# Small results of the sample's attention move to the three PSUM banks of the prompt's row maxima, and their own bank becomes a third bank of the prompt's scores

## The chip, the cores and the metric

The kernel runs on one core of a Trainium2 chip. The metric is the device time of one execution in microseconds (us), and of several runs the median. The core has TensorE (PE in the profile; its weight loads are a row of their own, PEld), VectorE (DVE), ScalarE (ACT), GpSimd (POOL) and SyncE (SP), whose queue issues nearly all transfers. Each engine works through its instructions in the order in which the program has them. A matrix product is written to PSUM, which has eight banks of 128 partitions by 512 fp32 numbers, and VectorE or ScalarE reads it from there.

## What is computed

One inference step of a small hybrid decoder, for a prompt of 2048 new tokens and for a sample batch of 8 sequences with 8 new tokens each and 4096 cached positions: a recurrent layer (RG-LRU), a shared key, value and forget stream, and one attention layer with 16 heads of 64. The change lies in the attention, whose core is

```
def fox_block(q, k, v, cq, ck, q_pos, k_pos):
    s = jnp.einsum('bqhd,bkhd->bhqk', q, k).astype(jnp.float32) * (HEAD_DIM ** -0.5)
    s = s + jnp.swapaxes(cq, 1, 2)[:, :, :, None] - jnp.swapaxes(ck, 1, 2)[:, :, None, :]
    mask = k_pos[None, :] <= q_pos[:, None]
    s = jnp.where(mask[None, None], s, -jnp.inf)
    p = jax.nn.softmax(s, axis=-1)
    return jnp.einsum('bhqk,bkhd->bqhd', p.astype(v.dtype), v)
```

For the prompt, k and v are its own 2048 rows. For the sample they are the cached pages (each of 128 rows, found through a page table) and the 8 new rows.

## The kernel before

**Stages.** The recurrent layer, the projections to q, k, v and the gate, and, from about 1708 us of the profiled execution on, the prompt's attention (the generator `attention`). It ends at about 2890 us, and the output projection (`project`) follows. The sample's attention (`decode`) runs beside the projections and beside the prompt's attention, up to about 2725 us: a `Side` object advances its generator by a share of the cost that the main generator reports, so the two are traced alternately. The framework's scheduler then makes each engine's order out of the traced order and its own model of when operands and buffers come free. That order is fixed in the program.

**The prompt's attention.** A unit is a head and a block of 512 queries, 64 units in all; even heads take their blocks in the order 0 to 3, odd heads in the order 3 to 0, so that a head has 4, 8, 12 and 16 key tiles, or the reverse: 640 key tiles in all. Four kinds of work make up a unit:

- *Maxima* (`top`, L1415 to L1419). For 128 queries and up to 512 keys a rough product goes to a bank `sx` (L1415). VectorE reduces it to a row maximum, with L1417, or with L1419 on the diagonal, which also adds the mask. A block's maxima are turned by a transpose (`mps`, L1432), and ScalarE writes them, negated, into rows 96 to 99 of the query tile `qbt` (L1434). Maxima are traced up to 18 key tiles (`LEAD`) ahead of the scores.
- *Scores* (`st`). Per key tile, two products into one bank: L1552 (`ka`, `qa`) and L1553 (`kbt`, `qbt`), which brings in the maxima and so needs the ScalarE rows. On the diagonal a third (L1555) adds the mask. ScalarE takes the exponential (L1561), into a tile `p`, or, for the first key tile of a unit, into a tile `acc`.
- *Products* (`ops`, L1572) of `p` and the values, after each four key tiles; GpSimd adds the `p` tiles up into `acc` (L106, the line of a helper).
- *Totals* (`tot`, L1465). After each four units, the four `acc` tiles are summed over partitions, which ends their use. There are 5 `acc` tiles. A total, a head's end (`rp`, L1489) and `mps` use banks of the tag `sx` too.

**The sample's attention.** A turn is one sequence and 8 heads, 16 turns in all, of which some ten lie beside the prompt's attention. Per turn, key pages arrive in `raw`, VectorE transposes them to `ktr` (L1168), and TensorE makes four sets of scores `dS` of 32 products each (L1136) and a small one for the new rows (L1151). VectorE subtracts the forget sums (`sc`, L106) and takes the maximum `gmx` (L1142). One bank `dm` then goes through a transpose (L1188), two VectorE steps (L1190, L1191), a product (L1192) and a VectorE copy (L1194). `dsum` (L1214) holds the softmax sums and `dres` (L1274) the turned result. The products with the value pages accumulate in a bank of their own, `dO` (L1246).

**Banks beside the prompt's attention.** Tag `st`: two. Tag `sx`: three. `ops`: one. Tag `d`: one, used in turn by `dS`, `dm`, `dsum` and `dres` through `bank`. Tag `o`: one, for `dO`. When `decode` has ended (`dec_done`), scores take the banks `d` and `o` as well, in the function `scores_bank`. A tag's tiles are given out in the traced order, each when the tile that had the bank is read out.

Of the kernel before, what the change touches and what calls it, by code (L numbers as in the profile page):

```python
# [11 lines left out]
F32 = mybir.dt.float32  # L12
# [8 lines left out]
P = 128  # L21
# [64 lines left out]
def tile_hawk_fox(  # L86
# [135 lines left out]
    psum = {}  # L222
# [810 lines left out]
    def decode(es, turns, nraw, nktr, ahead):  # L1033
# [26 lines left out]
        last, qbs = [], {}  # L1060

        def bank(name, tag="d"):
            return psum["dec"].tile([P, 512], F32, name=name, tag=tag, bufs=1)

        def spare():
# [52 lines left out]
        def keys(t, xs):  # L1118
# [11 lines left out]
            def scores(g, pp, kt):  # L1130

                sp = bank("dS", "d" if ahead or pp == 0 else "o")

                def score(h, x, a):
                    blk = (h * 2 + x) * 32
                    return T.matmul(sp[a * 32:(a + 1) * 32, h * P:(h + 1) * P], qw[:, pp * 2 + h // 2, h % 2 * 2 + x, :],  # L1136
                                    kt[:, :, a, blk:blk + 32], start=(x == 0), stop=(x == 1))

                together([partial(score, h, x, a) for h in range(4) for x in range(2) for a in range(4)], beside=True)
                sv = t.sc[:, g * 4:(g + 1) * 4, pp * 4:(pp + 1) * 4, :].rearrange("p n h i -> p h n i")  # L1140
                tt(V, sv, sp[:, :].rearrange("p (h n i) -> p h n i", h=4, n=4), sv, ALU.subtract)
                V.tensor_reduce(gmx[:, g, pp * 4:(pp + 1) * 4], sv, axis=AX.XY, op=ALU.max)  # L1142

            def new_scores(raw):
                kx = (spare() if ahead else pool.tile([P, 512], F32, name="kx", tag="kx"))[:, :512]
                V.transpose(kx, raw[:, :])
                sp = bank("dS")

                def score(h, x):
                    blk = (h * 2 + x) * 32  # L1150
                    return T.matmul(sp[:32, h * DS:(h + 1) * DS], qw[:, h // 2, h % 2 * 2 + x, :], kx[:, blk:blk + DS],  # L1151
                                    start=(x == 0), stop=(x == 1))

                together([partial(score, h, x) for h in range(8) for x in range(2)])
                tt(V, t.cn[:, :, :], sp[:DS, :64].rearrange("p (h j) -> p h j", h=8), t.cn[:, :, :], ALU.subtract)
                tt(V, t.cn[:, :, :], t.cn[:, :, :], maskN[:, :].unsqueeze(1).to_broadcast([DS, 8, DS]), ALU.add)
                V.tensor_reduce(gmx[:DS, 2, :], t.cn[:, :, :], axis=AX.X, op=ALU.max)
# [18 lines left out]
        def softmax(t):  # L1176
# [8 lines left out]

            V.tensor_reduce(mx[:, :8], gmx[:, :, :].rearrange("p g h -> p h g"), axis=AX.X, op=ALU.max)
            mp = bank("dm")
            T.transpose(mp[:, :P], mx[:, :], ident[:, :])  # L1188
            m1 = pool.tile([8, DS], F32, name="dm1", tag="dm1")
# [128 lines left out]
    def attention(es):  # L1318
# [215 lines left out]
        wide = [0]  # L1534

        def scores_bank():

            if dec_done:
                wide[0] += 1
                if wide[0] % 2:  # L1540
                    return psum["dec"].tile([P, 512], F32, name="st", tag="do"[wide[0] // 2 % 2], bufs=1)
            return ps3.tile([P, 512], F32, name="st", tag="st", bufs=2)

        for u, (h, qc) in enumerate(units):
            load_low(u + 2)
            for k in range(nks[u]):
                ka, kb = heads[h], kbs[h % 2]
                qa, qb = qas[u], qbs[u % NQ]
                lo = max(0, k - qc * 4) * P
                ks = slice(k * P, (k + 1) * P)  # L1550
                ps = scores_bank()
                place["T"] = T.matmul(ps[:, lo:], ka[:, ks], qa[:, lo:], start=True, stop=False).ins  # L1552
                T.matmul(ps[:, lo:], kb[:, ks], qb[:, lo:], start=False, stop=(k < qc * 4))  # L1553
# [201 lines left out]
    dec = ExitStack()  # L1755
# [47 lines left out]
    dec, att, last = ExitStack(), ExitStack(), ExitStack()  # L1803
# [56 lines left out]
```

## Time and profile before

| what | us |
|---|---|
| median of 3 runs | 3050.73 |
| the three runs | 3065.48, 3048.39, 3050.73 |
| the profiled execution | 3044.43 |
| its span in the profile | 3042.6 |
| busy in the span: PE, PEld | 2818.0, 2260.3 |
| busy: DVE, ACT, POOL | 1801.1, 1271.1, 1080.0 |

The profile is of one execution. Busy time of PE is that of matrix products with ends that are modelled, since they are pipelined, so that idle time of PE is a floor for what it loses. "A <- B: t, n, m" in the view of waits says that A's engine stood idle before A for t us in n places, at most m in one, until B was done. A stretch's PEclk is the clock that TensorE was granted, 1.00 being the full one. Instructions are named by line, engine, operation and tile, as in `L1552 PE MATMUL st<-qa,ka`.

### The profile page before, as it was taken

To read this page: it belongs to the slowest core of one execution; us is meant where nothing else is said; L and a number is where in the kernel's file an instruction comes from. 1 tells how busy PE (TensorE), PEld (TensorE's weight loads), DVE (VectorE), ACT (ScalarE), POOL (GpSimd) and SP (SyncE) were. 2 spreads that over 40 slices of the span, in tenths; PEclk is the share of its full clock that TensorE was granted. 3 is DMA by queue.
4 is the path that set the end of the run, shared out by engine and by line. 5 is a ranking of instruction groups with operands and counts; after the bars stand their busy time and mean duration, and the time that the engine had idled before them with its cause. 6 is when DMAs were issued, how large, how long until landed. Compare 5 with 4: busy or idle time off the path is not lost.

```text
span 3042.6 us, 60436 instructions
## 1 busy us (share of the span) xinstructions
PE 2818.0 (93%) x21614; PEld 2260.3 (74%) x21614; DVE 1801.1 (59%) x4012; ACT 1271.1 (42%) x2874; POOL 1080.0 (35%) x1199
## 2 busy tenths in 40 slices
PE   5998999999999989998999799899999999999998
PEld 5997789989899978896788455556655656556687
DVE  7876455425357765766555566666666766555344
ACT  4665442222236654433244144344434444355321
POOL 1653201000015532000000265556665666558422
PEclk9999999999999999999999799999999999999999
DMA  4224546788622265999999978898889898974343
GB/s 122 84 83 133 176 123 197 241 263 265 223 91 79 84 195 176 302 327 323 327 311 325 276 229 258 259 273 260 267 270 282 253 278 258 276 232 117 96 146 109
DMA packets 492862, 653.39 MB, mean 215 GB/s; under 512 B 91099, under 2 KB 292828, under 8 KB 485285
## 3 DMA queue, kind: packets, MB, share of 16 engines
q1 hardware_dynamic: 488934, 643.87, 67.8%
q10 hardware_dynamic: 3340, 3.56, 0.5%
q8 instruction: 171, 2.80, 0.4%
q0 software_dynamic: 288, 2.10, 0.2%
q14 instruction: 129, 1.06, 0.1%
HBM read 513.82 MB, written 135.16 MB: 213 GB/s over the span
## 4 chain that ended last, share of the span: by engine, by line
PE 51%; DMA 15%; DVE 6%; ACT 4%; SPq 4%; issue 3%; POOL 1%; ACTq 0%; DVEq 0%; POOLq 0%
PE ops L1572 7%; PE st L1552 4%; PE sx L1415 4%; DMA raw<-in_cache_k_dram 3%; PE dO L1246 3%; PE y L379 3%; PE y L378 3%; PE y L377 3%; PE kv L378 3%; PE kv L377 3%; PE st L1553 3%; PE kv L379 3%; PE dS L1136 3%; DMA raw<-in_cache_v_dram 3%; SPq L1083 2%
## 5 line engine op out<-in xcount | busy, mean ns | idle before, releaser
L106 POOL TENSOR_TENSOR acc<-acc,p 128x512 f32<-128x512 f32 (+3 forms) x576 | 639.7, 1112 | 408.2 <-PE ops L1572 220.6
L1561 ACT ACTIVATE p<-st 128x512 f32<-128x512 f32 (+3 forms) x576 | 291.5, 525 | 398.0 <-PE st L1553 183.9
L1168 DVE STREAM_TRANSPOSE ktr<-raw 128x1024 f32<-128x1024 f32 x256 | 308.0, 1226 | 107.2 <-DMA raw<-in_cache_k_dram 94.4
L1417 DVE TENSOR_REDUCE mxs<-sx 128x1 f32<-128x512 f32 x384 | 254.1, 681 | 183.2 <-PE sx L1415 182.0
L378 PE MATMUL kv<-wl,xh 128*128 128x256 f32 (+3 forms) x1088 | 310.0, 288 | 9.4 <-DVE wl L422 9.3
L377 PE MATMUL kv<-wh,xh 128*128 128x256 f32 (+3 forms) x1088 | 310.5, 290 | 6.9 <-ACT wh L421 6.6
L379 PE MATMUL kv<-wh,xl 128*128 128x256 f32 (+3 forms) x1088 | 309.8, 287 | 0.0
L1552 PE MATMUL st<-qa,ka 128*128 128x512 f32 (+3 forms) x640 | 273.1, 427 | 12.6 <-ACT p L1561 10.9
L1572 PE MATMUL ops<-p,vvt 128*64 128x256 f32 (+1 forms) x2176 | 269.1, 374 | 3.8 <-ACT p L1561 3.6
L1415 PE MATMUL sx<-kbt,qbt 96*128 96x512 f32 (+3 forms) x640 | 233.9, 421 | 34.8 <-DVE mxs L1419 12.7
L421 ACT ACTIVATE wh<-wst,gv 128x256 fp32r<-128x256 f32 (+1 forms) x384 | 164.3, 499 | 184.4 <-DMA wst<-in_b_w_in_dram 69.9
L1553 PE MATMUL st<-qbt,kbt 128*128 128x512 f32 (+3 forms) x640 | 238.1, 373 | 0.0
L422 DVE SCALAR_TENSOR_TENSOR wl<-wst,gv,wh 128x256 fp32r<-128x256 f32 (+1 forms) x384 | 170.2, 493 | 113.5 <-ACT wh L421 110.3
L1572 PEld LDWEIGHTS ops<-p,vvt 128*64 128x64 f32 x2176 | 165.0, 143 | 91.7 <-issue 22.2
L377 PE MATMUL qg<-xh,wh 128*128 128x384 f32 (+2 forms) x640 | 228.3, 358 | 0.0
L379 PE MATMUL qg<-xh,wl 128*128 128x384 f32 (+2 forms) x640 | 226.7, 355 | 1.1 <-DVE wl L422 1.1
L378 PE MATMUL qg<-xl,wh 128*128 128x512 f32 (+2 forms) x640 | 226.6, 356 | 0.0
L378 PEld LDWEIGHTS kv<-wl,xh 128*128 128x128 f32 (+1 forms) x1088 | 204.0, 189 | 13.9 <-DVE wl L422 10.9
L1101 POOL TENSOR_TENSOR qw<-qb,amask 128x128 f32<-128x128 f32 x64 | 29.4, 463 | 518.1 <-PE dS L1136 276.6
L377 PEld LDWEIGHTS kv<-wh,xh 128*128 128x128 f32 (+1 forms) x1088 | 203.8, 189 | 11.9 <-ACT wh L421 7.5
L379 PEld LDWEIGHTS kv<-wh,xl 128*128 128x128 f32 (+1 forms) x1088 | 205.7, 190 | 4.1 <-issue 3.9
L1552 PEld LDWEIGHTS st<-qa,ka 128*128 128x128 f32 x640 | 125.1, 196 | 107.4 <-issue 54.6
(297 smaller groups left out, 6346.4 us busy)
## 6 DMA issues: line engine op xcount, KB each, us to landing
raw<-in_cache_k_dram SPq DMA_DIRECT2D x512, 256.0 KB
raw<-in_cache_v_dram SPq DMA_DIRECT2D x512, 256.0 KB
wst<-in_w_kv_dram SPq DMA_DIRECT2D x48, 512.0 KB
wst<-in_b_w_in_dram SPq DMA_DIRECT2D x48, 512.0 KB
xt<-in_x_prompt_dram SPq DMA_DIRECT2D x32, 512.0 KB
wst<-in_a_w_in_dram SPq DMA_DIRECT2D x64, 256.0 KB
out_dram<-kf SPq DMA_DIRECT2D x128, 128.0 KB
sc<-cd SPq DMA_DIRECT2D x16, 1024.0 KB
```

Of the source, the lines that this page charges most:

```text
L106: eng.tensor_tensor(out, a, b, op=op)
L377: T.matmul(ps, lh(k), rh(k), start=(k == 0), stop=False)
L378: T.matmul(ps, lh(k), rl(k), start=False, stop=False)
L379: T.matmul(ps, ll(k), rh(k), start=False, stop=(k == nk - 1))
L422: V.scalar_tensor_tensor(wl[:, k, :], st[:, k, :], gk, f(wh[:, k, :]), op0=ALU.mult, op1=ALU.subtract)
L1168: behind("V", V.transpose(t.kts[pp][:, n], raw[:, :, pp * 256:(pp + 1) * 256]).ins)
L1415: T.matmul(ps[:, :w], qb[0:96, j * P:(j + 1) * P], kb[0:96, ck * 512:ck * 512 + w], start=True, stop=True)
L1417: place["V"] = V.reduce_max(mx[:, j, ck:ck + 1], ps[:, :w], axis=AX.X).ins
L1552: place["T"] = T.matmul(ps[:, lo:], ka[:, ks], qa[:, lo:], start=True, stop=False).ins
L1553: T.matmul(ps[:, lo:], kb[:, ks], qb[:, lo:], start=False, stop=(k < qc * 4))
L1561: pair.append((k, lo, p, A.activation(p[:, lo:], ps[:, lo:], AF.Exp)))
L1572: return T.matmul(ops[r * HD:(r + 1) * HD, a0 * P:], vvs[h % 2][:, k, :], p[:, :].rearrange("p (a r c) -> p a r c", a=2, r=2)[:, a0:, r, : ...
```

## The change

In `decode`, a bank of the tag `d` is now taken from the prompt's tag `sx` once the prompt's attention has its banks: `dS`, `dm`, `dsum` and `dres` stand in line with the maxima, `mps`, the totals and `rp` for three banks. In `scores_bank`, while `decode` runs, every third key tile takes the bank `d`, so that scores have three banks. After `decode` has ended, nothing differs.

```diff
         def bank(name, tag="d"):
+            if tag == "d" and "att" in psum:
+                return psum["att"].tile([P, 512], F32, name=name, tag="sx", bufs=3)
             return psum["dec"].tile([P, 512], F32, name=name, tag=tag, bufs=1)
...
                 wide[0] += 1
                 if wide[0] % 2:
                     return psum["dec"].tile([P, 512], F32, name="st", tag="do"[wide[0] // 2 % 2], bufs=1)
+            else:
+                wide[0] += 1
+                if wide[0] % 3 == 0:
+                    return psum["dec"].tile([P, 512], F32, name="st", tag="d", bufs=1)
             return ps3.tile([P, 512], F32, name="st", tag="st", bufs=2)
```

No instruction is added or taken away; those of the attention stand in another order. Lines of the changed kernel are higher by 2 in `decode` and `top`, by 6 from the score loop on (L1136 is L1138, L1415 is L1417, L1552 is L1558). The number behind a tile's name rises in the traced order, so that the same number is the same tile in both kernels.

**One set of the sample's scores among the maxima.** TensorE, some 170 key tiles into the prompt's attention; `dS_23166` is a set of the sample's scores, `sx` are maxima, `st` scores. Before:

```order
L1415 MATMUL sx_23210<-kbt0_19529,qbt0_19530 128x512
L1552 MATMUL st_23378<-qa_22786,ka_21615 128x256
L1553 MATMUL st_23378<-qbt3_19533,kbt1_19537 128x256
L1555 LDWEIGHTS identB_19558
L1555 MATMUL st_23378<-causal_19559,identB_19558 128x128
L1136 MATMUL dS_23166<-ktr_22732,qw_13815 32x128 x32
L1415 MATMUL sx_23231<-kbt0_19529,qbt0_19530 128x384
L1415 MATMUL sx_23234<-kbt0_19529,qbt0_19530 128x512
L1415 MATMUL sx_23258<-kbt0_19529,qbt0_19530 128x512
L1552 MATMUL st_23384<-qa_22786,ka_21615 128x128
```

And of the change, the same set of scores:

```order
L1417 MATMUL sx_23143<-kbt0_19529,qbt0_19530 128x256
L1138 MATMUL dS_23166<-ktr_22732,qw_13815 32x128 x32
L1417 MATMUL sx_23207<-kbt0_19529,qbt0_19530 128x512
L1417 MATMUL sx_23210<-kbt0_19529,qbt0_19530 128x512
L1417 MATMUL sx_23231<-kbt0_19529,qbt0_19530 128x384
L1417 MATMUL sx_23234<-kbt0_19529,qbt0_19530 128x512
L1417 MATMUL sx_23258<-kbt0_19529,qbt0_19530 128x512
L1248 MATMUL dO_23237<-raw_23448,sx_22996 32x256 x8
L1417 MATMUL sx_23261<-kbt0_19529,qbt0_19530 128x512
L1434 MATMUL mps_23271<-ident_92,mrow0_19567 128x128
L1153 MATMUL dS_23323<-sy_23321,qw_13815 32x8 x16
L1138 MATMUL dS_23343<-ktr_22733,qw_13815 32x128 x32
```

Before, the maxima 23207 and 23210 went ahead of the older `dS_23166`, and scores stood between. Now all users of the `sx` banks stand in the order of their numbers, and the maxima that were traced after `dS_23166` stand behind it in a row.

**The total that follows.** TensorE, a little later; `tot_23465` sums four `acc` tiles, and `st_23577` is a key tile's scores. Before:

```order
L1415 MATMUL sx_23436<-kbt0_19529,qbt1_19531 128x512
L1415 MATMUL sx_23459<-kbt0_19529,qbt1_19531 128x512
L1552 MATMUL st_23565<-qa_23277,ka_22541 128x512
L1553 MATMUL st_23565<-qbt5_19535,kbt0_19529 128x512
L1415 MATMUL sx_23462<-kbt0_19529,qbt1_19531 128x256
L1465 MATMUL tot_23465<-acc_22450,ones_97 32x512
L1465 MATMUL tot_23465<-acc_22791,ones_97 32x512
L1465 MATMUL tot_23465<-acc_23073,ones_97 32x512
L1465 MATMUL tot_23465<-acc_23283,ones_97 32x512
L1552 MATMUL st_23577<-qa_23277,ka_22541 128x512
```

And of the change:

```order
L1417 MATMUL sx_23433<-kbt0_19529,qbt1_19531 128x512
L1417 MATMUL sx_23436<-kbt0_19529,qbt1_19531 128x512
L1417 MATMUL sx_23459<-kbt0_19529,qbt1_19531 128x512
L1417 MATMUL sx_23462<-kbt0_19529,qbt1_19531 128x256
L1467 MATMUL tot_23465<-acc_22450,ones_97 32x512
L1467 MATMUL tot_23465<-acc_22791,ones_97 32x512
L1467 MATMUL tot_23465<-acc_23073,ones_97 32x512
L1467 MATMUL tot_23465<-acc_23283,ones_97 32x512
L1417 MATMUL sx_23479<-kbt0_19529,qbt1_19531 128x512
L1558 MATMUL st_23577<-qa_23277,ka_22541 128x512
```

Before, the scores of `st_23565` stood between the maxima that come ahead of the total; now those maxima stand in one row with it, and `st_23577` stands behind them.

**First and second halves of the scores.** TensorE, a little ahead of the first place; L1558 is the first product of a key tile's scores, L1559 the second, and `dres` the sample's turned result. In the kernel before, L1553 follows L1552 of the same key tile at all but a few places. Of the change:

```order
L1558 MATMUL st_23565<-qa_23277,ka_22541 128x512
L1434 MATMUL mps_23062<-ident_92,mrow1_19568 128x128
L1276 MATMUL dres_23088<-sel_13813,ob_23054 128x16 x4
L1417 MATMUL sx_23117<-kbt0_19529,qbt0_19530 128x512
L1417 MATMUL sx_23120<-kbt0_19529,qbt0_19530 128x512
L1417 MATMUL sx_23129<-kbt0_19529,qbt0_19530 128x128
L1559 MATMUL st_23506<-qbt5_19535,kbt0_19529 128x512
L1559 MATMUL st_23546<-qbt5_19535,kbt0_19529 128x512
L1559 MATMUL st_23565<-qbt5_19535,kbt0_19529 128x512
```

Three first halves stand ahead of the three second halves here, with maxima and a result of the sample between.

## The prediction

> **What bounds the kernel now.** I read the page first, then the stretches around the change, then the waits inside the one it touches, and last its groups of instructions. The stretches are: up to the prompt's attention, the attention with the sample beside it, the attention alone, the output projection.
>
> ```profile
> span 3042.6 us, 60436 instructions
> core 0: us, PE busy (x) PEld busy (x) DVE busy (x) ACT busy (x) POOL busy (x), PEclk, DMA share, GB/s
> 0.00:1708.00 1708.00, 1577.15 (x11656) 1441.08 (x11656) 1011.92 (x2258) 723.18 (x1547) 345.64 (x513) 0.97 0.64 204
> 1708.00:2725.00 1017.00, 939.59 (x8479) 599.08 (x8480) 647.80 (x1372) 439.43 (x1094) 585.50 (x563) 0.94 0.86 264
> 2725.00:2890.00 165.00, 158.38 (x864) 104.81 (x864) 77.30 (x174) 79.58 (x169) 113.73 (x95) 0.98 0.38 107
> 2890.00:3043.00 153.00, 142.87 (x618) 115.36 (x616) 64.04 (x210) 28.88 (x64) 35.13 (x29) 0.98 0.39 127
> ```
>
> Only the second line can change: before it the sample still has its own bank, after it the order of banks is the old one. In its 1017 us PE is busy for 939.6, so 77.4 us of idle time, and what a slower clock costs, is all there is to win. VectorE, with 647.8, has room on the average; whether it has it at the right moment is the question. The waits in this stretch:
>
> ```profile
> PEld st L1552 <- ACT p L1561: 36.9, 81, 2.6
> ...
> PE dO L1246 <- DMA raw<-in_cache_v_dram: 19.9, 10, 5.2
> ...
> PEld sx L1415 <- DVE mxs L1419: 19.1, 23, 5.6
> ...
> PEld sx L1415 <- DVE mxs L1417: 14.1, 31, 1.5
> PE sx L1415 <- DVE mxs L1419: 12.7, 12, 5.1
> ...
> PE st L1552 <- ACT p L1561: 10.9, 24, 2.3
> ...
> ACT acc L1561 <- PE tot L1465: 7.0, 6, 3.0
> ...
> PE mps L1432 <- DVE mrow L1428: 5.2, 5, 2.7
> ...
> PE sx L1415 <- DVE mxs L1417: 4.2, 8, 1.0
> ```
>
> A score that waits for the exponential of an earlier one wants a bank: that is the wait that the change goes for, and it is small. Maxima that wait for VectorE want a bank of the three that now get more users: 12.7, 4.2 and 5.2 us together, already twice as much. The longest wait, for value pages, has nothing to do with banks.
>
> **The bank gained (term A).** A third bank for 553 key tiles. PE stands idle 10.9 us for want of one. Its weight load waits 36.9 us, but mostly while the product before it is still in the array. The gain is at least about 3 us, if most of these waits are for a ScalarE that is simply behind, and at most 36.9 + 10.9 = 47.8. I take 15, near the row for PE itself, and allow a little for weight loads that come late.
>
> **The banks shared: room.** Per turn the maxima's banks take over four sets `dS`, a small one, `dm`, `dsum` and `dres`. Room alone is not the problem: a set is 64 rows of PE and one VectorE step, about 2.7 us, ten turns have forty of them, and the stretch has 3 x 1017 us of bank time. `dm` is the longest, because it is passed between PE and VectorE three times. Its first and last instruction, in one turn and in another:
>
> ```profile
> L1188 PE MATMUL dm<-ident,dmx x1: 271/271/271, 1977.0 to 1977.0; 128*128 128x128 f32 x1
> L1194 DVE COPY dnm<-dm x1: 160/160/160, 1981.0 to 1981.0; 128x8 f32<-128x8 f32 x1
> ...
> L1188 PE MATMUL dm<-ident,dmx x1: 273/273/273, 2464.9 to 2464.9; 128*128 128x128 f32 x1
> L1194 DVE COPY dnm<-dm x1: 159/159/159, 2474.9 to 2474.9; 128x8 f32<-128x8 f32 x1
> ```
>
> So `dm` holds its bank for 4 to 10 us, in which the maxima have two left.
>
> **The banks shared: order (term B).** What costs is that banks of a tag go out in the traced order. In the order before, I compared each result of the sample with its number: it stood up to 14 users of the `sx` banks ahead of its place, up to 12 behind. Now all stand at it, so a set that is late for its pages holds up every maximum behind it, and these then come in a row, at VectorE's pace and not at PE's. I counted rows of four or more maxima with no score or product of the prompt between, without the 19 at the start: 11 rows with 54 maxima before, 21 with 135 now. Of 640 second halves of scores, 5 had another key tile's first half open before, 58 now: they wait for maxima. What a maximum costs on the two engines, and what the sample adds on VectorE:
>
> ```profile
> L1417 DVE TENSOR_REDUCE mxs<-sx 128x1 f32<-128x512 f32 x344 | 227.7, 680 | 162.5 <-PE sx L1415 161.5
> ...
> L1415 PE MATMUL sx<-kbt,qbt 96*128 96x512 f32 (+2 forms) x577 | 212.2, 423 | 33.9 <-DVE mxs L1419 12.7 <-DMA raw<-in_cache_v_dram 11.4 <-DVE mxs L1417 4.2
> ...
> L1168 DVE STREAM_TRANSPOSE ktr<-raw 128x1024 f32<-128x1024 f32 x150 | 181.7, 1227 | 27.0 <-DMA raw<-in_cache_k_dram 18.4 <-DMA qa<-qd 4.4 <-issue 3.8
> ...
> L1419 DVE CUSTOM_DVE_ANT_0 sx<-sx,maskb 128x128 f32<-128x128 f32 x233 | 111.5, 486 | 60.7 <-PE sx L1415 57.6 <-PE dm L1192 1.3 <-PE st L1552 1.0
> ...
> L1419 DVE DVE_READ_ACCUMULATOR2_ANT mxs<- 128x1 f32 x233 | 31.7, 136 | 0.0
> ...
> L106 DVE TENSOR_TENSOR sc<-dS,sc 128x512 f32<-128x512 f32 x38 | 26.1, 688 | 48.4 <-PE dS L1136 48.4
> L1142 DVE TENSOR_REDUCE gmx<-sc 128x4 f32<-128x512 f32 x38 | 25.6, 673 | 0.2
> ```
>
> A maximum is (227.7 + 111.5 + 31.7) / 577 = 0.64 us on VectorE and 212.2 / 577 = 0.37 on PE, 0.27 apart. 81 more of them in rows: 22 us. With three banks the first two or so of each of the ten new rows cost nothing, 20 x 0.27 = 5 less: 17. VectorE's own order puts transposes (1.23 each) and the sample's steps between; laying all that it does between a row's first and last maximum against PE's work there, with the means of such rows, PE comes out 29 us short in all rows before and 55 now, 26 more. Before, PE's idle time for maxima was 12.7 + 4.2 + 5.2 = 22.1, three quarters of the 29. So I take 20. The bounds are 0, if other work of PE covers it, and 55, if each new wait costs in full.
>
> **Totals (term C).** At an odd head's end the units are short and the fifth `acc` is taken quickly; the sixth has to wait for a total. ScalarE's 7.0 us in 6 places is that wait. The total now stands behind whatever the sample holds up, as in the second place shown, some seven times. While the exponential into `acc` is parked, its score holds one bank of the three: part of A is given back here. I take 6 us, about as much again as today; the bounds are 0 and 30, seven waits of the longest kind in these rows, 4 to 5 us.
>
> **Nothing from the rest.** The sample ends 9 key tiles later in the order (its last `dres` stands at tile 561, before at 552); at 1017 / 553 = 1.84 us each that is 17 us, which lie under the 165 us of attention that follow. What is behind it, the splitting of the output weights, is late by as much and not yet needed. SP's queue has the page loads in nearly the same places between the prompt's loads (0 to 2 query loads apart), so I cost it at nothing; without that cover it would show in the wait for value pages.
>
> **The clock (term D).** An idle PE also loses afterwards:
>
> ```profile
> 2404.79 0.33 PE L1432 MATMUL mps<-ident,mrow 128*128 128x128 f32 x1 [2.68 <-DVE mrow L1428]
> ...
> 2400.00:2404.80 4.80, 2.12 (x17) 1.29 (x18) 3.20 (x7) 1.93 (x4) 1.19 (x2) 1.00 0.90 275
> 2404.80:2413.00 8.20, 8.20 (x83) 6.76 (x83) 3.80 (x14) 2.30 (x6) 0.00 (x0) 0.58 1.01 253
> 2413.00:2420.00 7.00, 7.00 (x102) 5.19 (x104) 4.50 (x14) 3.50 (x8) 5.65 (x5) 1.00 1.03 354
> ```
>
> After 2.68 us of waiting for a block's maxima, the next 8.2 us ran at 0.58, so some 3.4 us went on top. Over the stretch a clock of 0.94 costs 0.06 x 939.6 = 56 us beside 77 of idle time, 0.7 per us of it. A + B + C is -15 + 20 + 6 = 11; at 0.7, D is 7 or 8.
>
> [...]
>
> **Sum.** 11 + 7 = 18 us. The profiled execution took 3044.4, so 3062 in its terms. It lies 6.3 under the median of the runs, 3050.7, in whose terms the forecast is 3069, slower by 0.6%.
>
> **Rivals.** *The third bank decides.* PE's order is fixed and the rows of maxima stand where the scheduler's model had waits; the chip may have none there, as VectorE is idle 36% of the stretch. Then B and C go to 0 and A to about half of its 47.8, and with fewer gaps the clock helps a little: about -21, 3030. For it: 81 waits of weight loads for a bank against 54 for the maxima's. Against it: those rows have PE hardly idle. [...]
>
> *Gain and loss cancel.* A at 15 and B + C at the lower half, 10 to 20: within 5 us, 3052. For it: everything stands in tens of microseconds beside 3050. It is also the case in which the third bank is seldom of use, since the tag `d` has one bank and a key tile whose turn it is waits for just that one.
>
> *The sample sets the pace.* Its chain (maximum, `dm`, `dsum`, transposes, products with values) can no longer run ahead, and each of ten turns waits four or five times for a maximum's bank, at 1 to 1.5 us each: 40 to 75 us, and pages are freed later by as much. It decides once the sample ends after the prompt, whose lead is 165 us; before that, PE only feels it through its fixed order. About +60, 3111. Against it: the sample ends just 9 tiles later.
>
> **How the numbers follow.** The forecast has 0.53, the third bank 0.23, cancelling 0.17, the sample's pace 0.07. The forecast's own range is 3056 to 3100: A from 15 to 25, B from 12 to 40, C to 15, with the clock. For the whole, 3028 takes in about half of the second case, 3112 most of the last. A change of 0.5%, 15 us, is about what can be told from none: below 3035.5 is faster, above 3066 slower. Faster is the second case, 0.23; slower most of the first and the last, 0.50; within, the rest, 0.27.
>
> **What would show it.** In the stretch with the sample: `st` <- ACT p on PE down from 10.9 to under 4 (A); `sx` <- DVE and `mps` <- DVE up from 22 to about 40 (B); ACT acc <- PE tot up (C); PEclk at 0.93 or less (D); stretches before 1708 the same to within 3 us. I am wrong if idle time for maxima stays near 22, if the wait for value pages moves by more than 10 us, or if the stretch's length changes and the idle rows don't say why.

## The result, and the profile after

The change makes the kernel slower: 3176.2 us median (3164.7 to 3181.6, 4 runs) against 3049.6 of the kernel before in the same job, a ratio of 1.041 (95% interval 1.038 to 1.044), some 127 us. The direction was forecast; the size forecast was 18 us, and the time lies far outside the range (to 3112).

The same four stretches of the changed kernel; its second one ends with the last product of the sample. Columns as before: the stretch, its length, busy time of PE, PEld, DVE, ACT, POOL with their instructions, granted clock, DMA share, GB/s.

```profile
span 3169.6 us, 60443 instructions
...
0.00:1708.00 1708.00, 1574.96 (x11657) 1440.01 (x11658) 1011.78 (x2258) 723.97 (x1547) 345.41 (x513) 0.97 0.65 204
1708.00:2842.00 1134.00, 979.91 (x8472) 623.99 (x8472) 647.95 (x1364) 429.01 (x1093) 585.55 (x563) 0.89 0.77 235
2842.00:3017.00 175.00, 162.28 (x872) 107.47 (x871) 81.17 (x182) 79.49 (x172) 109.42 (x95) 0.94 0.38 109
3017.00:3170.00 153.00, 143.18 (x619) 115.62 (x617) 64.44 (x210) 28.88 (x64) 35.46 (x29) 0.98 0.39 128
```

Of the 127 us that the span has grown, 117 are in the stretch with the sample (1017 to 1134), 10 in the attention alone, which was forecast to stay, and none ahead or behind. In the stretch VectorE, ScalarE and GpSimd do the same work in about the same time (DVE 647.8 before, 648.0 now; ACT 439.4 and 429.0). PE's idle time rises from 77.4 to 154.1, and its busy time by 40.3 for the same products: the granted clock falls from 0.94 to 0.89. Idle time, and the busy time that a slower clock stretches, are the 117 us.

The waits of PE in this stretch (idle time of the engine named first, in us, then how often and the longest):

```profile
PE dO L1248 <- DMA raw<-in_cache_v_dram: 70.9, 27, 8.2
PE mps L1434 <- DVE mrow L1430: 28.9, 15, 4.6
...
PE dS L1138 <- DVE ktr L1170: 10.7, 4, 4.0
PE sx L1417 <- DVE mxs L1419: 9.7, 20, 0.8
...
PE st L1558 <- ACT p L1567: 4.8, 6, 2.7
PE sx L1417 <- DVE mxs L1421: 2.7, 6, 0.9
```

The wait that the change goes for did shrink, from 10.9 us to 4.8. Two others have grown far more: for the value pages, 19.9 to 70.9, and for a block's maxima to be ready for their transpose, 5.2 to 28.9. The waits of `sx` for a bank have fallen from 16.9 to 12.4. From the same view for ScalarE and for VectorE:

```profile
ACT acc L1567 <- PE tot L1467: 56.4, 6, 15.0
```

```profile
DVE sc L106 <- PE dS L1138: 101.9, 37, 8.2
```

The exponential into a fresh `acc` waits 56.4 us for a total, in six places, which cost 7.0 before; and VectorE waits 101.9 us for the sample's scores (48.4 before), which now stand in one line with the maxima.

The sample as a whole, by the products with its value pages; duration of one in ns (least, median, most), first and last start in us. Before, then after:

```profile
L1246 PE MATMUL dO<-raw,sx x1408: 376/379/637, 1724.3 to 2722.1; 128*32 128x256 f32 x176
```

```profile
L1248 PE MATMUL dO<-raw,sx x1408: 376/379/637, 1722.9 to 2838.8; 128*32 128x256 f32 x176
```

The same 1408 products, as fast at the median, take 1115.9 us from first to last instead of 997.8. The prompt's attention is spread over the longer stretch with them, because PE's order interleaves the two.

### The profile page after: what moved, and what is told of

Its sections match the earlier page's. It is cut to its first block, busy times and chain, and to the rows that moved or that the text cites. A ratio compares the mean times of both kernels' runs of the same rounds, so it can differ in the third digit from the quotient of the medians.

```text
span 3169.6 us, 60443 instructions
## 1 busy us (share of the span) xinstructions
PE 2860.3 (90%) x21614; PEld 2287.1 (72%) x21614; DVE 1805.3 (57%) x4012; ACT 1261.3 (40%) x2874; POOL 1075.8 (34%) x1199
## 4 chain that ended last, share of the span: by engine, by line
PE 51%; DMA 16%; DVE 6%; SPq 4%; ACT 3%; issue 3%; POOL 1%; ACTq 0%; DVEq 0%; POOLq 0%
PE ops L1578 6%; DMA raw<-in_cache_v_dram 5%; PE st L1558 4%; PE dO L1248 4%; PE dS L1138 3%; PE kv L378 3%; PE kv L377 3%; PE kv L379 3%; PE st L1559 3%; PE sx L1417 3%; PE y L378 3%; PE y L377 3%; PE y L379 3%; SPq L1085 2%; DMA raw<-in_cache_k_dram 2%
## 5 line engine op out<-in xcount | busy, mean ns | idle before, releaser
L1567 ACT ACTIVATE p<-st 128x512 f32<-128x512 f32 (+3 forms) x576 | 282.2, 525 | 371.6 <-PE st L1559 194.7
L1170 DVE STREAM_TRANSPOSE ktr<-raw 128x1024 f32<-128x1024 f32 x256 | 308.2, 1226 | 75.1 <-DMA raw<-in_cache_k_dram 70.9
L1417 PE MATMUL sx<-kbt,qbt 96*128 96x512 f32 (+3 forms) x640 | 243.6, 438 | 31.7 <-DMA qbt<-qd 11.8
L1558 PE MATMUL st<-qa,ka 128*128 128x512 f32 (+3 forms) x640 | 266.3, 420 | 6.4 <-ACT p L1567 4.8
L1559 PE MATMUL st<-qbt,kbt 128*128 128x512 f32 (+3 forms) x640 | 235.9, 382 | 1.8 <-ACT qbt L1436 1.8
L1248 PE MATMUL dO<-raw,sx 128*32 128x256 f32 x2048 | 154.1, 425 | 85.9 <-DMA raw<-in_cache_v_dram 72.8
L377 PEld LDWEIGHTS kv<-wh,xh 128*128 128x128 f32 (+1 forms) x1088 | 204.2, 189 | 11.5 <-ACT wh L421 7.2
```

The lines of the kernel that those rows point to most:

```text
L377: T.matmul(ps, lh(k), rh(k), start=(k == 0), stop=False)
L1170: behind("V", V.transpose(t.kts[pp][:, n], raw[:, :, pp * 256:(pp + 1) * 256]).ins)
L1248: return T.matmul(op[c:c + 32, :256], sx[:, d, i // 4, a * 4:(a + 1) * 4, :].rearrange("p h q -> p (h q)"), raw[:, d, a * 256:(a + 1) * 25 ...
L1417: T.matmul(ps[:, :w], qb[0:96, j * P:(j + 1) * P], kb[0:96, ck * 512:ck * 512 + w], start=True, stop=True)
L1567: pair.append((k, lo, p, A.activation(p[:, lo:], ps[:, lo:], AF.Exp)))
```

## The experiments

Each is timed against the kernel before in its own job (medians there 3048 to 3054). For every kernel I also took two numbers from PE's fixed order, as the prediction did for two. *Rows*: how many maxima stand in rows of four or more with no score or product of the prompt between. This count does not take the third product of a diagonal key tile for a break; it gives 58 for before, where the prediction counted 54, and 135 for the change. *Lead*: how many key tiles ahead of its unit's scores a block's maxima are transposed, on the mean: 8.2 before, 1.4 in the change.

### The change in two halves

The shared line alone, scores with two banks, the bank `d` empty beside the prompt's attention:

```diff
         def bank(name, tag="d"):
+            if tag == "d" and "att" in psum:
+                return psum["att"].tile([P, 512], F32, name=name, tag="sx", bufs=3)
```

> The sample's small results use the maxima's three banks, as in the change; scores keep two banks, and the bank d stands empty beside the prompt's attention. If the loss comes from the small results standing in the maxima's line (my theory now: the sample can no longer run ahead, its key pages hold their buffers longer, and value pages are asked for too late), nearly all of it is here: 3140 to 3190 us, PE's wait for value pages 50 us or more in the stretch with the sample, time from the dm copy to dsum about 20 us against 10 before. If the third bank of the scores is what harms (scores run ahead of their maxima and push them back), the time is near that before: 3045 to 3075.

Measured: 3112.0, ratio 1.020 (1.017 to 1.023). The line costs 61 us by itself, and the third bank of scores, which was to pay for it, another 64 on top. Its stretch and three of its waits on PE:

```profile
1708.00:2790.00 1082.00, 964.97 (x8477) 604.71 (x8480) 644.88 (x1360) 436.05 (x1091) 589.31 (x566) 0.92 0.81 246
```

```profile
PE dO L1248 <- DMA raw<-in_cache_v_dram: 43.8, 22, 7.1
PE st L1554 <- ACT p L1563: 19.9, 39, 1.7
...
PE sx L1417 <- DVE mxs L1421: 4.5, 9, 0.9
```

From this kernel to the change the scores' wait for a bank falls by 15.1 us, and the kernel is 64 us slower.

The scores' third bank without the line: the sample keeps `d`, and the maxima give up one of their three banks.

```diff
-            ps = ps3.tile([P, 512], F32, name="sx", tag="sx", bufs=3)
+            ps = ps3.tile([P, 512], F32, name="sx", tag="sx", bufs=2)
...
-            return ps3.tile([P, 512], F32, name="st", tag="st", bufs=2)
+            return ps3.tile([P, 512], F32, name="st", tag="st", bufs=3)
```

> The small results keep their own bank d; scores get three banks of their own and the maxima two. If a third bank for the scores is worth the 11 to 48 us that stood as waits for an exponential before, and two banks do for the maxima when nothing of the sample stands among them, 3020 to 3050 us. If the maxima need the third bank (they wait for VectorE some 0.65 us each), slower than before: 3060 to 3110 us.

Measured: 3188.9, 1.044 (1.042 to 1.047). Two things move here, so the control is the first of them alone: two banks for the maxima, two for the scores, one bank empty.

> The kernel before with two banks of maxima in place of three; one bank stands empty. It is e3 without its third bank of scores. In the order the lead is 2.0 tiles, against 0.6 in e3 and 8.2 before. If the lead decides, 3130 to 3185 us, and e3's third bank adds little to it; if the third bank of the scores harms by itself as much as from e1 to the change (64 us), about 3125 or less.

Measured: 3192.4, 1.046 (1.044 to 1.048), the same within 4 us. A third bank for the scores is worth nothing there; the third bank of the maxima is worth 140 us. The stretch with the sample in this kernel, with maxima in two banks, and five of its waits on PE:

```profile
1708.00:2858.00 1150.00, 995.15 (x8453) 609.93 (x8455) 645.83 (x1356) 437.03 (x1089) 590.13 (x569) 0.90 0.77 233
```

```profile
PE dO L1246 <- DMA raw<-in_cache_v_dram: 59.5, 28, 8.0
PE sx L1415 <- DVE mxs L1417: 21.7, 40, 2.0
PE st L1552 <- ACT p L1561: 14.4, 32, 1.8
...
PE mps L1432 <- DVE mrow L1428: 9.4, 8, 3.2
...
PE sx L1415 <- DVE mxs L1419: 5.3, 11, 0.8
```

Here nothing of the sample stands in the maxima's line, and yet the value pages come late as in the change, and the clock falls as far. The waits of `sx` for a bank are only 10.1 us longer (27.0 after 16.9), and the stretch is 133 us longer: what a shortage of maxima's banks costs does not stand in the wait for these banks.

### What the line costs: room, order, and which tiles

Maxima and small results in one line again, but with four banks, `d` as the fourth; scores with two:

```diff
+    def ring4(name):
+        turn4[0] += 1
+        if turn4[0] % 4 == 0:
+            return psum["dec"].tile([P, 512], F32, name=name, tag="d", bufs=1)
+        return psum["att"].tile([P, 512], F32, name=name, tag="sx", bufs=3)
...
-            ps = ps3.tile([P, 512], F32, name="sx", tag="sx", bufs=3)
+            ps = ring4("sx") if not dec_done else ps3.tile([P, 512], F32, name="sx", tag="sx", bufs=3)
```

> The maxima and the small results share four banks in one line (the three of the maxima and d in turn), scores keep two: as many banks in all as before, and only the line is common. If the loss is the common line, it stays for the most part: 3110 to 3180 us. If it is that three banks are too few for both, it goes: 3045 to 3070 us.

Measured: 3070.8, 1.006 (1.004 to 1.008). With as many banks as before, standing in one line costs about 18 us; the bank that is missing in the shared line costs the other 41 to 43.

Only the sets of scores `dS` in the line (`name == "dS"` in the condition of `bank`), then only the rest:

> Only the sample's scores dS use the maxima's banks; dm, dsum and dres keep the bank d, and scores have two banks. If the loss is by way of the key pages (dS late, so ktr and raw are held longer), at least two thirds of it is here: 3130 us or more, key pages held near 30 us against 23 before. If it is by way of the softmax chain (dm, dsum, dres made to wait), at most a third: under 3095 us.

> The counterpart of e4: dS keeps the bank d, and dm, dsum and dres use the maxima's banks; scores have two. What I now hold to be the cause is read off TensorE's order: by how many key tiles the turned maxima (mps) of a unit stand ahead of that unit's scores, on the mean. It is 8.2 before, 8.0 with e2 (3071), 5.6 with e4 (3074), 4.0 with e1 (3112), 1.4 in the change (3176), 0.6 with e3 (3189). Here it is 6.0, so by this theory 3065 to 3080 us. If dS and the rest each carried half of e1's 61 us, 3085 or more.

Measured: 3074.0, 1.007 (1.005 to 1.010), and 3063.2, 1.004 (1.002 to 1.005). Together 34 us, little more than half of the 61 that both cost in one kernel: either kind alone leaves the other a bank of its own. In the second of the two, `dsum` follows `dnm` by 20.0 us on the mean, as in the change (20.9; before, 10.3), and that kernel is only 13 us slower.

### Is it the lead of the maxima?

The kernel before with `LEAD` cut from 18 to 6:

> All banks as before; only the maxima are traced 6 key tiles ahead at most in place of 18. In the order the turned maxima then stand 4.0 tiles ahead on the mean, as in e1. If the lead is what is lost with the change, this is slower by much of what e1 is: 3085 to 3125 us, PE's waits for mrow up. If the banks and their common line are the cause and the lead only goes with them, 3045 to 3065 us.

Measured: 3100.2, 1.016 (1.014 to 1.019), lead 4.0, rows 71. A short lead costs by itself: PE's wait of `mps` for `mrow` goes from 5.2 to 29.7 us here, as in the change.

The shared line without the third bank, and `LEAD` 8, which brings the lead to 1.5, that of the change:

> As e1 (small results in the maxima's line, two banks of scores, d empty), with the maxima traced 8 key tiles ahead at most in place of 18. In the order the turned maxima stand 1.5 tiles ahead, as with the change (1.4). If the change's third bank of scores does its harm by way of the lost lead alone, this comes out where the change does, 3150 to 3190 us, with both marks: PE's wait for value pages 50 us or more and mps for mrow 20 or more. If the third bank harms in another way, well under it: 3100 to 3140.

Measured: 3117.7, 1.022 (1.020 to 1.024), rows 68. Only 6 us more than the line with `LEAD` 18, and 58 short of the change. The theory that the third bank harms by the lead alone fell. PE's waits differ too: 43.3 us of `mps` for `mrow` and 19.3 for value pages here, 3.0 and 43.8 with the line and `LEAD` 18.

### Halves, priority and queues

The change with the second product of a key tile first, so that no half-made score holds a bank while it waits for the maxima:

```diff
-                place["T"] = T.matmul(ps[:, lo:], ka[:, ks], qa[:, lo:], start=True, stop=False).ins
-                T.matmul(ps[:, lo:], kb[:, ks], qb[:, lo:], start=False, stop=(k < qc * 4))
+                place["T"] = T.matmul(ps[:, lo:], kb[:, ks], qb[:, lo:], start=True, stop=False).ins
+                T.matmul(ps[:, lo:], ka[:, ks], qa[:, lo:], start=False, stop=(k < qc * 4))
```

> The change, with the two products of a key tile's scores in the other order: the one that needs the maxima comes first, so that a score takes its bank only when its maxima are there. In the order one key tile is left whose halves stand apart, against 58 in the change, and the lead is 1.7 tiles against 1.4. If banks held by half-made scores are what harms in the change, 3080 to 3130 us; if it is the lost lead, 3155 to 3185 us, as the change.

Measured: 3168.3, 1.038 (1.035 to 1.041). Second halves behind another open half fall from 58 to 2, and the time by 8 us only. Half-made scores were not the cause; the line with `LEAD` 8 has 83 such second halves and is 58 us faster than the change.

The kernel before with the maxima's products put first by the scheduler (`with tc.high_priority():` around `top(u, j, ck)`):

> All banks as before; the scheduler is told to prefer the maxima to the scores. The lead in the order is 10.0 tiles against 8.2. If lead is time all along the scale, 3030 to 3048 us; if more than some 8 is of no use, 3045 to 3060.

Measured: 3068.0, 1.006 (1.004 to 1.008), slower and outside both expected ranges: the lead rises to 10.0, but rows to 91.

The prompt's loads on ScalarE's queue in place of SP's (`queue[0] = S` left out), in the change and in the kernel before, to see whether SP's queue lets the pages come late:

> The change, with the prompt's loads of keys, values and queries issued by ScalarE's queue in place of SP's, so that they do not stand among the sample's page loads. If value pages come late because SP's queue is held up by those loads (L1405 waits 76 us in the change, 34 before), PE's wait for value pages falls from 71 to under 45 us and the time to under 3150. If pages are late because the sample's own work comes late, it stays: 3155 to 3185.

> The kernel before, with the same loads on ScalarE's queue: the counterpart of e11. If SP's queue costs there too, 3025 to 3045 us; otherwise 3045 to 3060.

Measured: 3212.3, 1.052 (1.049 to 1.055), and 3123.2, 1.023 (1.021 to 1.025). The move costs 70 us in the kernel before, 36 in the change. With SP's queue free of these loads in both, the wait for value pages in the change falls from 70.9 to 42.5, but the change is still 89 us slower than the kernel before. So most of the 127 us is not the work of SP's queue; whether the other 38 are can't be told from two kernels that the move itself slows.

### Rows against lead, and the dose

What still lay open were the 64 us of the third bank. Three kernels set rows, lead and the turn of the single bank against each other. The change with the third bank for every sixth key tile:

```diff
-                if wide[0] % 3 == 0:
+                if wide[0] % 6 == 0:
```

> The change, but only every sixth key tile takes the third score bank, not every third. In its order 98 maxima stand in rows of four or more (change 135, the shared line without the third bank 78), and blocks of maxima are turned 1.9 key tiles ahead of their scores (change 1.4, line alone 4.0). If the 64 us between the line alone (3112) and the change (3176) come from maxima that are bunched in rows: about a third to a half of them, 3130 to 3145. If they come from the lost lead: nearly all of them, 3165 to 3175. If each turn of the single bank costs by itself: half, 3144.

Measured: 3138.5, 1.030 (1.027 to 1.033): 27 of the 64 us at half the dose (31 by the ratios). The change with `LEAD` 12:

> The change with maxima traced 12 key tiles ahead of the scores, not 18. In its order 112 maxima stand in rows (change 135), but their lead is 1.0 key tile (change 1.4). If the rows decide: faster than the change by 15 to 40 us, 3135 to 3160. If the lead decides: slower than the change, 3180 to 3200. If each turn of the single bank costs: as the change, 3170 to 3182.

Measured: 3154.6, 1.035 (1.032 to 1.038), faster than the change although its maxima come later. The change with the maxima's products put first:

> The change with the rough products of the maxima given first place by the scheduler where it may choose. In its order 144 maxima stand in rows (change 135), their lead is 2.2 key tiles (change 1.4), and 45 second halves of scores have another first half open (change 58). If the rows decide: no better than the change, 3175 to 3190. If the lead decides: faster, 3145 to 3165. If each turn of the single bank costs: as the change, 3170 to 3182.

Measured: 3181.4, 1.044 (1.040 to 1.047), no better than the change although its lead is longer. In all three the range for the rows held; the lead missed all three, the turn of the single bank the second.

The waits on PE at half the dose lie between those of the line alone and those of the change:

```profile
PE dO L1248 <- DMA raw<-in_cache_v_dram: 56.0, 24, 9.0
PE mps L1434 <- DVE mrow L1430: 18.7, 12, 4.5
PE st L1558 <- ACT p L1567: 15.7, 27, 3.1
```

But rows don't order all kernels. The table has rows, lead, two waits of PE in the stretch with the sample, and the time for which a set of key pages is held, from the issue of its first load to the end of the second transpose of it; times are in us, the lead in key tiles.

| kernel | time | rows | lead, tiles | value pages | `mps` for `mrow` | hold |
|---|---|---|---|---|---|---|
| before | 3050 | 58 | 8.2 | 19.9 | 5.2 | 23.3 |
| `LEAD` 6 | 3100 | 71 | 4.0 | 4.1 | 29.7 | 19.9 |
| line alone | 3112 | 78 | 4.0 | 43.8 | 3.0 | 27.6 |
| line, `LEAD` 8 | 3118 | 68 | 1.5 | 19.3 | 43.3 | 22.5 |
| change, `LEAD` 12 | 3155 | 112 | 1.0 | 33.4 | 62.1 | 28.3 |
| change, halves swapped | 3168 | 161 | 1.7 | 70.0 | 28.5 | 30.6 |
| change | 3176 | 135 | 1.4 | 70.9 | 28.9 | 30.3 |
| two banks of maxima, three of scores | 3189 | 161 | 0.6 | 52.8 | 12.5 | 34.7 |
| two banks of maxima | 3192 | 115 | 2.0 | 59.5 | 9.4 | 32.9 |

Swapping the halves brings 26 more maxima into rows and the time falls by 8 us; the third bank of scores beside two of maxima brings 46 more, and the time stays.

Last, the sample's key pages, whose hold is the last column. It rises from before to the line, to the change and to the kernels with two maxima's banks, but not everywhere with the time: with `LEAD` 6, and with the line and `LEAD` 8, it is below that of the kernel before, and these are 50 and 65 us slower. To pull it down, `with tc.high_priority():` around VectorE's transposes (L1170), in the change and in the kernel before:

> The change with VectorE's transposes of the sample's key pages given first place by the scheduler where it may choose, so that pages should be let go sooner; PE's order keeps 143 maxima in rows of four or more (change 135). If the key pages held by late transposes are what makes the change slow (held 30 us on the mean from first issue to second transpose, 23 before): 3110 to 3150, with the hold near 26. If the rows of maxima decide and the hold only follows them: 3170 to 3190, hold near 30.

> The same edit in the kernel before, as the control: 61 maxima in rows of four or more (before 58). If rows decide: 3045 to 3060. If an earlier transpose is worth time by itself: 3025 to 3045.

Measured: 3170.1, 1.039 (1.036 to 1.042), and 3044.1, 0.997 (0.996 to 0.999). The time in the change is what rows foretell, but the hold did not come down (30.7), so the run says nothing on the hold as a cause. In the kernel before, the edit gives the one version found that is not slower, by a quarter of a per cent; that is at the edge between the 3045 to 3060 which rows foretold and the 3025 to 3045 for an earlier transpose, so it tells neither.

## Why the prediction was right and wrong

Two steps of the prediction failed: room, which it put at nothing, and term A, which it put at 15 us won.

**Term A, the third bank: right as a wait, wrong as time.** The wait of scores for ScalarE fell to 4.8 (forecast: under 4), by 6.1. That it fell by 15.1 from the line alone, where the wait had grown first, is the 15 of the forecast by chance. The step took the wait that went away for time that is won. In the fixed order other waits grew, and the third bank costs 64 us beside the line and gains nothing clear (under 4 us) beside two maxima's banks. The wait went from 19.9 with the line alone to 4.8, and no run here shows time won by it; here the bank came out of the room of another line.

**The step that failed first: "Room alone is not the problem."** It set forty holds of 2.7 us against 3 x 1017 us of bank time, an average. The runs show the opposite: one bank of three taken from the maxima costs 140 us though VectorE was busy for 64% of the stretch, and of the line's 61 us the missing bank makes 41 to 43 and the common line at equal room 18. So term B, forecast at 20 for order alone, left out the larger part. That its 20 is near the 18 is luck: it was worked out from 81 more maxima in rows, and the kernel with four banks in one line has 12 more.

**Term B, where it shows.** I had it in waits of `sx` for VectorE, up to about 40 with `mps`. The sum is 9.7 + 2.7 + 28.9 = 41.3, the number forecast, but by luck, since it is in another place: `sx` waits went down, and the 28.9 are blocks whose last maximum had only just been reduced, a wait for data and not for a bank. The count of maxima in rows describes the times, with the lead beside it. Over the 17 kernels with the prompt's loads on SP's queue (before and the change among them), the line that fits best is 3085 us + 0.75 per maximum in rows - 9.6 per key tile of lead. By it the line alone has 55 us to pay (61 measured), the third bank on top 68 (64), `LEAD` 6 in the kernel before 50 (50). It is a description fitted to these same times, off by up to 24 us, and by some 43 for two maxima's banks (3149 for 3192), the slowest kernel with the prompt's loads there; between the kernels named under the table it goes the wrong way. The prediction priced a maximum in a row at 0.27, what VectorE takes longer than PE. What it costs by this fit is nearly three times that; the sample's transposes and scores, which stand behind the row, may be why, but no run shows it.

**Term C, totals: mis-sized.** 6 was put, at most 30; ScalarE's wait went from 7.0 to 56.4, in as many places, at 9.4 each instead of 1.2. The bound took "seven waits of the longest kind" from the kernel before, in which no total stood behind a held line. Little of it seems to reach the end: the change with `LEAD` 12 has 4.9 us of this wait and is only 22 us faster, and the kernel with only `dm`, `dsum` and `dres` in the line has 30.1 and is 13 us slower than before. It wasn't tried by itself.

**"Nothing from the rest": failed.** The wait for value pages went from 19.9 to 70.9, far over the 10 us named as the sign of being wrong. The reason given, that SP's order has hardly changed, is true and beside the point. Loads are issued in order, but when a buffer comes free (SP's page loads wait for products with value pages 27.9 us in 11 places before, 37.2 in 22 in the change), and each turn of the sample runs slower. In the change the products with a set of value pages start 9.2 us after the issue of the set's last load on the mean (median 7.0), 11.5 before (9.7), so that more of the transfer lies open; and `dsum` follows `dnm` 21 us later instead of 10. The later `dsum` costs little by itself, as the kernel with only the rest in the line shows. All this is near the rival "the sample sets the pace", which was given 0.07 and was to decide only once the sample ends after the prompt. That condition was needless: in the change the sample ends 175 us ahead of the prompt's attention, and PE, in its fixed order, stood idle for 70.9 us before the sample's value pages. The rival's 60 us of price would do for the line alone, not for the change.

**Term D, the clock: right in kind.** 0.7 us of slower clock per us of idle time was put; 40.3 / 76.7 = 0.5 was measured. It was small only because A + B + C were. The trace has PE's clock at 0.50 in 18 spells, 99 us in all, of this stretch before, and in 31, 236 us, in the change. The longest idle time of PE, as the profile models it, that reaches into the 9 us ahead of a spell is anything from 0.6 to 5.2 us before and from 0.7 to 8.2 us in the change, so the runs show no one length of idle time at which the clock falls.

**The other rivals.** "The third bank decides" and "cancel" both took A for time won; the runs leave nothing of either. Two sums don't come out, and neither bears on the miss: the bounds given for the forecast's own range make 3029 to 3119 with the clock, not 3056 to 3100, and half of 47.8, helped by the clock, is a gain of more than 24, not of 21.

**What stays open.** How the third bank costs its 64 us. Rows and a short lead go with the time in dose and sign for most kernels, with the exceptions above, and no run shows the path by which a row becomes late pages; the hold does not rise with every loss. Wherever banks were changed the order changed with them, because the scheduler makes the order from its model of when banks come free. No run has the old order with fewer banks, so what a missing bank costs on the chip and what the new order costs are not separated. The change with the maxima put first also shows a limit of the idle time as a measure: its stretch with the sample is

```profile
1708.00:2865.00 1157.00, 1028.95 (x8464) 621.84 (x8464) 653.08 (x1360) 430.56 (x1094) 585.78 (x563) 0.91 0.76 231
```

PE is idle for 128 us there, less than the change's 154, in a longer stretch and at a higher clock. PE is busy there for 1029.0 us with about as many products as in the change, for 979.9 in the change at the lower clock. Busy time of PE is modelled, and some of its standing still seems to be counted as busy; these two kernels can't be ranked by their idle time. More buffers for the pages, the direct test of the hold, were not tried.

## What to carry to other kernels

Before a buffer moves from one line of tiles to another, ask what its old line loses, not only which wait the new one drops: the test is to take the buffer away and leave it empty (here 140 us lost, against a wait of 11 us to be won). Average room says little where tiles go out in one traced order; count in the new order how many users of the line come in a row, and how far ahead of their consumers they stand, but take the count for a description until a run separates it from the rest. And where one engine's fixed order holds two streams, a stream that runs later can make the other late long before it would end last (here 70.9 us of waiting for value pages, with the sample's end 175 us ahead of the prompt's).

## What the runs showed of the hardware

Loads issued on ScalarE's queue held up its exponentials. With the prompt's loads there, in the kernel before, the trace of the stretch with the sample has 175 issues of loads on ScalarE, 125 us in all (4 and 6 us without the move), and PE waits for it:

```profile
PE ops L1571 <- ACT p L1560: 40.0, 22, 9.0
PE st L1551 <- ACT p L1560: 37.4, 26, 8.4
```

Before these were 3.6 and 10.9, and the waits for value pages shrank meanwhile from 19.9 to 7.9: 70 us lost for 12 us of waiting saved. And products of the same shape became slower on the mean, with more idle time around them: with the clock at 0.89 for 0.94, one product with a value page takes 438 ns, before 406, and one of the sample's scores 315, before 284. The groups of instructions of the kernel before, then of the change:

```profile
L1246 PE MATMUL dO<-raw,sx 128*32 128x256 f32 x1408 | 99.9, 406 | 20.0 <-DMA raw<-in_cache_v_dram 19.9
L1136 PE MATMUL dS<-ktr,qw 128*32 128x128 f32 x2432 | 78.3, 284 | 6.6 <-DVE cn L106 3.8 <-DVE ktr L1168 2.6
```

```profile
L1248 PE MATMUL dO<-raw,sx 128*32 128x256 f32 x1408 | 110.4, 438 | 72.6 <-DMA raw<-in_cache_v_dram 70.9 <-issue 1.3
L1138 PE MATMUL dS<-ktr,qw 128*32 128x128 f32 x2432 | 92.4, 315 | 10.7 <-DVE ktr L1170 10.7
```
